# Last pair of a feed-forward stage: the first pair's squares moved behind its first plain chunk, its two token halves swapped, one PSUM bank taken from a fresh tile

## Chip, core and metric

The kernel runs on one core of one Trainium2 chip. The metric is the device time of one execution in microseconds (us). All work is in float32, but TensorE is fed float32r operands: each float32 operand is split into a rounded part ("hi", names `wh`, `act`, and half of `g` and `gs`) and the rest ("lo", `wl`), and a product is made of three matmuls: hi by hi, hi by lo, lo by hi.

## What is computed

One decoder layer on 256 tokens of width 2048. Only its end matters here: a squared-ReLU MLP of width 8192, a normalisation over the row, and a residual sum.

```
u = rms_norm(h, pre_ff_gain[l], NORM_EPS)
f = jnp.square(jax.nn.relu(u @ w_ff1[l])) @ w_ff2[l]
h = h + rms_norm(f, post_ff_gain[l], NORM_EPS)
```

The row's mean square needs all 2048 columns of `f`, so the last step can't begin before the last column block is there.

## The kernel before

Tokens come in two halves of 128 (`t` = 0, 1). The MLP's hidden width is done in four quarters `q`; in each, 16 column chunks of `w_ff1` give `g`, and then `w_ff2` is applied in two passes `fast_pair(ga, q, m)`, each for a pair of column blocks of 512 (block 2m + i, i = 0, 1). So `m` = 0 is the first pair, `m` = 1 the last, and the last pass of all (`q` = 3, `m` = 1) is called closing.

A pass has, along the quarter's hidden width, four chunks `kc` of 512. Chunks `kc` = 0 and 1 are done as a **unit** (`fast_unit`): a 2 x 2 block scheme with seven products, named A1 to A7, in place of eight. A unit takes 42 matmuls: three operand buffers of 12 (A1 and A2, A7 and A3, A5 and A6) and one of 6 (A4). Chunks `kc` = 2 and 3 are done plainly, 24 matmuls each for one column block (`plain_chunk`, 12 for each token half). The closing pass has its own order: unit 0, then the plain chunks (2,0) and (3,0) of column block i = 0, then unit 1, then both plain chunks of block i = 1, token half by token half.

The operands come from HBM into three `raw` buffers of 1 MB (queue of SP, line 134) and from there into three pairs of `wh` and `wl` buffers: ScalarE casts raw to `wh` (L140 a whole chunk, L156 half a buffer of a unit), VectorE subtracts for `wl` (L146, L157). A unit's buffers are partly sums of raw blocks (VectorE, L162). A raw buffer is loaded again as soon as VectorE has read it last.

In every pass but the closing one, the two plain column blocks of the result are copied by ScalarE to `tmp` and added to the total (`acc`, in the trace `y_sb`) by DMAs with accumulation that GpSimd issues (L859); the unit's part goes the same way from `ev` (L816). In the closing pass VectorE adds directly (L814, L833, L866).

`finish(n, t, ...)` takes the square of one 128 x 512 block of the total with its row sum (ScalarE, L873) and then multiplies the block by the gain (VectorE, L876). For the last block it also takes the root (L875) and the reciprocal (L878), and the final loop (L914, one per block) scales, adds the residual, and stores (SP, L916). Before the change the four `finish` calls of the first pair stand in the program right after `fast_pair(ga, 3, 0)`; where each engine runs them is the scheduler's choice, as `finish` doesn't pin its instructions to their place in the program.

Results lie in PSUM tiles `ps` of two banks each. Four tiles, `pa` to `pd`, fill PSUM. In the closing pass the last column block has both halves in the two banks of `pd`: `plain[1, 1]` is bank 0, `plain[0, 1]` is bank 1. Each engine runs its own list in order, and an instruction that waits holds up those behind it.

Of the kernel before, what the change touches and what calls it, by code (L numbers as in the profile page):

```python
# [13 lines left out]
AF = mybir.ActivationFunctionType  # L14
# [6 lines left out]
NT = S // P  # L21
# [16 lines left out]
NQ = 4  # L38
# [8 lines left out]
FAST = 2  # L47
# [8 lines left out]
def tile_layer(ctx, tc, x, x_t, pre, vecs, lams, rope_t, subln, b_conv, post_mix, post_ff,  # L56
               w_q, w_k, w_v, w_cv, w_cg, w_ga, w_gc, w_co, w_o, w_f1, w_f2, out):
    nc = tc.nc
# [46 lines left out]
    pin = tc.keep_in_program_order  # L105
# [103 lines left out]
    def take():  # L209
        if not queue:  # L210
            fill()
        return queue.pop(0)

    def done(refill=True):
        state["live"] -= 1
        if refill:
            fill()
# [34 lines left out]
    def new_ps():  # L252
        pi[0] += 1
        return ps_pools[pi[0] % len(ps_pools)].tile([P, 2, 512], F32, name="ps")
# [497 lines left out]
    acc = y_sb  # L752
# [20 lines left out]
    def fast_pair(ga, q, m):  # L773
# [64 lines left out]
        for kc, i in chunks:  # L838
            if kc < FAST:
                if i == 0:  # L840
                    fast_unit(kc, kc == FAST - 1)
                    if kc == FAST - 1:
                        combine()
                        if closing:
                            first_half()
                continue
            if closing and i == 1:
                continue
            wt = take()
            for t in (1, 0):  # L850
                plain_chunk(kc, i, wt, t)
            done()
            if (kc, i) != [c for c in plains if c[1] == i][-1]:
                continue
            if not closing:
                tmp = evp.tile([P, NT, 512], F32, name="tmp", bufs=2)
                for t in (1, 0):
                    nc.scalar.copy(tmp[:, t], plain[t, i])
                    nc.gpsimd.dma_start(total(t, i), tmp[:, t], accum_op=ALU.add)  # L859
        if closing:  # L860
            wts = [take(), take()]
            for t in range(NT):
                for j in range(2):
                    plain_chunk(FAST + j, 1, wts[j], t)
                with tc.high_priority(offset=CHAIN):
                    nc.vector.tensor_tensor(total(t, 1), plain[t, 1], total(t, 1), op=ALU.add)  # L866
                    finish(2 * m + 1, t, total(t, 1), True)
            done()
            done()

    def finish(n, t, dst, last):
        sq = fin2.tile([P, 2, S], F32, name="z").rearrange("p a t -> p (a t)")
        nc.scalar.activation(sq, dst, AF.Square, accum_out=fss[:, t, n:n + 1])  # L873
        if last:
            nc.scalar.activation(r3[:, t:t + 1], fss[:, t, n:n + 1], AF.Sqrt, bias=fpre[:, t:t + 1], scale=1.0 / D)  # L875
        nc.vector.tensor_tensor(dst, dst, pff[n // 2][:, (n % 2) * 512:(n % 2 + 1) * 512], op=ALU.mult)  # L876
        if last:
            nc.vector.reciprocal(r3[:, t:t + 1], r3[:, t:t + 1])  # L878

    for q in range(NQ):  # L880
        ga = Mixed()
        for j in range(KT // 2):
            ps = ws_pair(u2) if q or j else lead_ps
            z = fin2.tile([P, 2, S], F32, name="z")
            ws_sum(z, ps)
            nc.vector.tensor_tensor(z, z, r2b.unsqueeze(1).to_broadcast([P, 2, S]), op=ALU.mult)
            sc = fin2.tile([P, 8, P], F32, name="sc", bufs=1)
            gg = sc[:, 0:4].rearrange("p (a t) n -> p a (t n)", a=2)
            nc.vector.scalar_tensor_tensor(gg, z, 0.0, z, op0=ALU.max, op1=ALU.mult)
            if j < 2 * FAST:  # L890
                ga.put_fast(j, sc)
            else:
                ga.put_pair(j, gg)
        if q == NQ - 1:
            def again():
                return actp.tile([P, 2, 2 * S], F32R, name="act").bitcast(F32)

            pff = [again().rearrange("p a n -> p (a n)") for i in range(2)]
            for i in range(2):
                nc.gpsimd.dma_start(pff[i], post_ff[i * 1024:(i + 1) * 1024].partition_broadcast(P))  # L900
            h_fin = [again() for n in range(NB)]
            for n in range(NB):
                nc.gpsimd.dma_start(h_fin[n], h_keep[:, :, n * 512:(n + 1) * 512])
        for m in range(NB // 2):
            fast_pair(ga, q, m)
            if q == NQ - 1 and m == 0:
                for n in range(2):
                    for t in range(NT):
                        finish(n, t, acc[:, t, n * 512:(n + 1) * 512], False)
    out_r = out.rearrange("(t p) d -> p t d", p=P)  # L910
    for t in range(NT):
        for n in range(NB):
            ns = slice(n * 512, (n + 1) * 512)
            nc.vector.scalar_tensor_tensor(acc[:, t, ns], acc[:, t, ns], r3[:, t:t + 1], h_fin[n][:, t],  # L914
                                           op0=ALU.mult, op1=ALU.add)
            nc.sync.dma_start(out_r[:, t, ns], acc[:, t, ns])  # L916
# [64 lines left out]
```

## Time and profile before

| | us |
|---|---|
| three runs: median (lowest to highest) | 1551.09 (1549.72 to 1553.07) |
| profiled execution: its own time | 1549.57 |
| profiled execution: span of the trace | 1547.8 |
| TensorE busy in the span | 1524.4 |
| VectorE busy | 1274.6 |
| ScalarE busy | 787.0 |
| GpSimd busy | 41.8 |

The span runs from the first to the last instruction; the execution's own time has 1.8 us more around it. Times in the trace count from the start of the span. The closing pass begins at 1485.3 and the span ends at 1547.8. A busy TensorE row is a matmul in the pipeline: a matmul of 512 columns shows 0.39 us, but the next starts 0.23 us after it.

### The profile page before, as it was taken

How to read it: one execution, taken by the hardware profiler on the slowest of the kernel's cores; microseconds unless marked ns; L12 is line 12 of the kernel's file. 1: busy time of each engine (PE TensorE's matmuls, PEld its weight loads, DVE VectorE, ACT ScalarE, POOL GpSimd, SP SyncE). 2: the span in 40 equal slices, each digit the busy share in tenths (PEclk: the TensorE clock that was granted, in tenths of full speed). 3: DMA queues.
4: the chain of work that ended last, by engine and by line, in shares of the span. 5: the costliest groups of instructions: out<-in, count | busy, mean ns of one | idle time of the engine just before them, and what ended most of it. 6: DMA issues, size and time to landing. Idle time of an engine off the chain costs nothing. (4 is left out here: it accounts for less than half of the span.)

```text
span 1547.8 us, 19432 instructions
## 1 busy us (share of the span) xinstructions
PE 1524.4 (98%) x7734; PEld 1297.3 (84%) x7734; DVE 1274.6 (82%) x1605; ACT 787.0 (51%) x851; POOL 41.8 (3%) x73
## 2 busy tenths in 40 slices
PE   9999999999999999999999999999999999999986
PEld 8888888888888888888887888888888888888865
DVE  7999999999999997956546878867887778867877
ACT  7444454555555545734436545554455445544553
POOL 0000000000000000000000000000011000100010
PEclk9999999999999999999999999999999999999999
DMA  8655555454545555575555754775388546885672
GB/s 305 217 190 189 189 191 188 165 189 164 190 163 178 203 192 192 187 274 188 190 190 172 250 190 167 240 245 189 144 267 268 213 172 195 262 257 189 240 217 95
DMA packets 51484, 313.66 MB, mean 203 GB/s; under 512 B 5825, under 2 KB 5953, under 8 KB 16705
## 3 DMA queue, kind: packets, MB, share of 16 engines
q1 hardware_dynamic: 43920, 289.61, 52.3%
q0 software_dynamic: 7040, 22.02, 6.0%
q8 instruction: 60, 0.98, 0.2%
q10 hardware_dynamic: 432, 0.79, 0.2%
q14 instruction: 32, 0.25, 0.0%
HBM read 295.62 MB, written 4.19 MB: 194 GB/s over the span
## 5 line engine op out<-in xcount | busy, mean ns | idle before, releaser
L140 ACT CAST wh<-raw 128x2048 fp32r<-128x2048 f32 (+2 forms) x260 | 460.8, 1778 | 492.4 <-PE ps L294 162.6
L146 DVE TENSOR_TENSOR wl<-raw,wh 128x2048 fp32r<-128x2048 f32 (+2 forms) x260 | 552.0, 2127 | 192.5 <-ACT wh L140 188.3
L271 PE MATMUL ps<-act,wh 128*128 128x512 f32 x1984 | 479.2, 392 | 0.3 <-ACT wh L140 0.3
L271 PEld LDWEIGHTS ps<-act,wh 128*128 128x128 f32 x1984 | 364.6, 188 | 70.8 <-ACT wh L140 0.6
L275 PEld LDWEIGHTS ps<-act,wl 128*128 128x128 f32 x1984 | 256.6, 191 | 10.0
L275 PE MATMUL ps<-act,wl 128*128 128x256 f32 x1984 | 264.0, 284 | 0.0
L293 PE MATMUL ps<-wl,act 128*128 128x512 f32 x624 | 243.8, 391 | 0.0
L292 PE MATMUL ps<-wh,act 128*128 128x512 f32 x624 | 243.7, 390 | 0.0
L294 PE MATMUL ps<-wh,act 128*128 128x512 f32 x624 | 243.6, 390 | 0.0
L478 DVE SCALAR_TENSOR_TENSOR y_all<-c,vec,y_all 128x256 f32<-128x256 f32 x480 | 210.8, 483 | 0.0
L293 PEld LDWEIGHTS ps<-wl,act 128*128 128x128 f32 x624 | 117.2, 188 | 24.2
L294 PEld LDWEIGHTS ps<-wh,act 128*128 128x128 f32 x624 | 117.2, 188 | 24.1
L292 PEld LDWEIGHTS ps<-wh,act 128*128 128x128 f32 x624 | 117.1, 188 | 23.9
L156 ACT CAST wh<-raw 128x1024 fp32r<-128x1024 f32 x64 | 65.3, 1050 | 91.8 <-PE ps L829 26.0
L828 PE MATMUL ps<-wl,g 128*128 128x512 f32 x256 | 101.5, 397 | 1.1
L827 PE MATMUL ps<-wh,g 128*128 128x512 f32 x256 | 100.0, 390 | 2.2 <-DVE y_sb L866 2.2
L829 PE MATMUL ps<-wh,g 128*128 128x512 f32 x256 | 99.7, 389 | 0.0
L797 PE MATMUL ps<-wh,gs 128*128 128x512 f32 x224 | 87.8, 392 | 5.5 <-ACT wh L156 5.5
L798 PE MATMUL ps<-wl,gs 128*128 128x512 f32 x224 | 87.9, 393 | 0.5 <-DVE wl L157 0.5
L800 PE MATMUL ps<-wh,gs 128*128 128x512 f32 x224 | 87.6, 391 | 0.0
L157 DVE TENSOR_TENSOR wl<-raw,wh 128x1024 fp32r<-128x1024 f32 x64 | 76.4, 1221 | 2.2 <-PE ps L275 1.1
L156 ACT CAST wh<-sum 128x1024 fp32r<-128x1024 f32 x48 | 49.1, 1050 | 38.6 <-PE ps L271 14.3
(200 smaller groups left out, 1257.2 us busy)
## 6 DMA issues: line engine op xcount, KB each, us to landing
raw<-in_w_f_dram SPq DMA_DIRECT2D x124, 1024.0 KB, 5.0
raw<-in_w_q_dram SPq DMA_DIRECT2D x16, 1024.0 KB, 4.9
raw<-in_w_k_dram SPq DMA_DIRECT2D x16, 1024.0 KB, 4.8
raw<-in_w_v_dram SPq DMA_DIRECT2D x16, 1024.0 KB, 4.8
raw<-in_w_ga_dram SPq DMA_DIRECT2D x16, 1024.0 KB, 4.8
raw<-in_w_gc_dram SPq DMA_DIRECT2D x16, 1024.0 KB, 4.8
raw<-in_w_co_dram SPq DMA_DIRECT2D x16, 1024.0 KB, 4.9
raw<-in_w_o_dram SPq DMA_DIRECT2D x16, 1024.0 KB, 4.9
```

Source lines behind the costliest of these rows:

```text
L140: i = nc.scalar.copy(wh[:, a:b], raw[:, a:b])
L146: i = (eng or nc.vector).tensor_sub(wl[:, a:b], raw[:, a:b], wh[:, a:b].bitcast(F32))
L156: nc.scalar.copy(hi, src)
L271: a = nc.tensor.matmul(ps[:, j], wh[:, k * P:(k + 1) * P], acts.both(k), start=(k == 0), stop=False)
L275: a = nc.tensor.matmul(ps[:, j, S:], wl[:, k * P:(k + 1) * P], acts.hi(k), start=False, stop=(k == KT - 1))
L292: nc.tensor.matmul(ps, acts.hi(k, a, b), wh[:, sl], start=(k == 0), stop=False)
L293: nc.tensor.matmul(ps, acts.hi(k, a, b), wl[:, sl], start=False, stop=False)
L294: nc.tensor.matmul(ps, acts.lo(k, a, b), wh[:, sl], start=False, stop=(k == KT - 1))
L478: i = nc.vector.scalar_tensor_tensor(y, c[:, j:j + S], vcol(ct, V_DW + j), y, op0=ALU.mult, op1=ALU.add)
L827: pin(nc.tensor.matmul(ps, ga.hi(k, a, b), wh[:, sl], start=first, stop=False))
L828: pin(nc.tensor.matmul(ps, ga.hi(k, a, b), wl[:, sl], start=False, stop=False))
L829: pin(nc.tensor.matmul(ps, ga.lo(k, a, b), wh[:, sl], start=False, stop=last))
```

## The change

Three edits, all around the closing pass. First, the four `finish` calls of the first pair are made inside the closing pass, after its first plain chunk (2,0), and the squares are pinned to that place. Second, the last column block is done with token half 1 first, and the final loop runs over the halves in the same order. Third, `plain[0, 1]` is a bank of a fresh PSUM tile, which takes the place of `pa` once that has been read.

```
             done()
+            if closing and kc == FAST:
+                for n in range(2):
+                    for t in range(NT):
+                        finish(n, t, acc[:, t, n * 512:(n + 1) * 512], False, pinned=True)
...
         if closing:
+            plain[0, 1] = new_ps()[:, 0]
             wts = [take(), take()]
-            for t in range(NT):
+            for t in (1, 0):
                 for j in range(2):
                     plain_chunk(FAST + j, 1, wts[j], t)
...
-    def finish(n, t, dst, last):
+    def finish(n, t, dst, last, pinned=False):
         sq = fin2.tile([P, 2, S], F32, name="z").rearrange("p a t -> p (a t)")
-        nc.scalar.activation(sq, dst, AF.Square, accum_out=fss[:, t, n:n + 1])
+        i = nc.scalar.activation(sq, dst, AF.Square, accum_out=fss[:, t, n:n + 1])
+        if pinned:
+            pin(i)
...
             fast_pair(ga, q, m)
-            if q == NQ - 1 and m == 0:
-                for n in range(2):
-                    for t in range(NT):
-                        finish(n, t, acc[:, t, n * 512:(n + 1) * 512], False)
     out_r = out.rearrange("(t p) d -> p t d", p=P)
-    for t in range(NT):
+    for t in (1, 0):
```

Lines behind the first edit have other numbers in the changed kernel: L866 is L871, L873 is L878, L876 is L883, L914 is L917.

ScalarE's list, before, from the last casts of unit 0 to those of unit 1. The cast from `sum` that stands alone between two pairs of squares is A4's of unit 0; the two casts of 128 x 2048 are the chunks (2,0) and (3,0); the four casts from `raw` behind them and the three from `sum` are unit 1's.

```order
L156 CAST wh<-sum 128x1024
L873 ACTIVATE z,fss<-y_sb 128x512 x2
L156 CAST wh<-sum 128x1024
L140 CAST wh<-raw 128x2048 x2
L156 CAST wh<-raw 128x1024 x2
L873 ACTIVATE z,fss<-y_sb 128x512 x2
L156 CAST wh<-raw 128x1024 x2
L156 CAST wh<-sum 128x1024 x3
```

The same place in the changed kernel:

```order
L156 CAST wh<-sum 128x1024 x2
L140 CAST wh<-raw 128x2048 x2
L156 CAST wh<-raw 128x1024 x3
L878 ACTIVATE z,fss<-y_sb 128x512 x3
L156 CAST wh<-raw 128x1024
L878 ACTIVATE z,fss<-y_sb 128x512
L156 CAST wh<-sum 128x1024 x3
```

No square stands ahead of A4's cast any more, nor ahead of the two chunks. All four now stand among unit 1's casts: three ahead of the fourth raw cast (operand A7), one behind it.

VectorE's list, before, from the second half of A4's sums to the last subtraction of unit 1; the L876 are the gain products behind the four squares.

```order
L157 TENSOR_TENSOR wl<-sum,wh 128x1024 x2
L876 TENSOR_TENSOR y_sb<-y_sb,act 128x512 x2
L157 TENSOR_TENSOR wl<-sum,wh 128x1024
L146 TENSOR_TENSOR wl<-raw,wh 128x2048 x2
L157 TENSOR_TENSOR wl<-raw,wh 128x1024 x2
L876 TENSOR_TENSOR y_sb<-y_sb,act 128x512 x2
L162 TENSOR_TENSOR sum<-raw 128x1024
L157 TENSOR_TENSOR wl<-raw,wh 128x1024
L162 TENSOR_TENSOR raw<-raw 128x2x512
L162 TENSOR_TENSOR sum<-raw 128x1024
L157 TENSOR_TENSOR wl<-raw,wh 128x1024
L162 TENSOR_TENSOR sum<-sum,raw 128x1024
```

The same place in the changed kernel:

```order
L157 TENSOR_TENSOR wl<-raw,wh 128x1024 x2
L162 TENSOR_TENSOR sum<-raw 128x1024
L162 TENSOR_TENSOR raw<-raw 128x2x512
L157 TENSOR_TENSOR wl<-raw,wh 128x1024
L883 TENSOR_TENSOR y_sb<-y_sb,act 128x512
L162 TENSOR_TENSOR sum<-raw 128x1024
L883 TENSOR_TENSOR y_sb<-y_sb,act 128x512 x2
L157 TENSOR_TENSOR wl<-raw,wh 128x1024
L883 TENSOR_TENSOR y_sb<-y_sb,act 128x512
L162 TENSOR_TENSOR sum<-sum,raw 128x1024
L157 TENSOR_TENSOR wl<-sum,wh 128x1024 x3
```

All four gain products now stand between unit 1's sums and subtractions; before, two stood ahead of A4's subtraction of unit 0 and two ahead of unit 1's first sum.

VectorE's end, before, from the scale of the first three squares' sums on:

```order
L836 TENSOR_SCALAR fpre<-fpre 128x2
L878 RECIPROCAL r_6985<-r_6985 128x1
L914 SCALAR_TENSOR_TENSOR y_sb<-y_sb,r_6985,act 128x512 x4
L866 TENSOR_TENSOR y_sb<-ps,y_sb 128x512
L876 TENSOR_TENSOR y_sb<-y_sb,act 128x512
L878 RECIPROCAL r_6985<-r_6985 128x1
L914 SCALAR_TENSOR_TENSOR y_sb<-y_sb,r_6985,act 128x512 x4
```

And in the changed kernel:

```order
L836 TENSOR_SCALAR fpre<-fpre 128x2
L871 TENSOR_TENSOR y_sb<-ps,y_sb 128x512
L885 RECIPROCAL r_6985<-r_6985 128x1
L917 SCALAR_TENSOR_TENSOR y_sb<-y_sb,r_6985,act 128x512 x4
L883 TENSOR_TENSOR y_sb<-y_sb,act 128x512
L885 RECIPROCAL r_6985<-r_6985 128x1
L917 SCALAR_TENSOR_TENSOR y_sb<-y_sb,r_6985,act 128x512 x4
```

The sum that takes the last half out of PSUM (L866, now L871) moves from behind the first half's four final operations to ahead of them and of their reciprocal. TensorE's list has the same rows in the same order; what its first matmul of the last half waits for is VectorE's L809 (the last reader of `pa`) where it was L866 (the reader of the other bank of `pd`).

## Rows read from the trace of the kernel before

**Rows 1.** The page, part 1: busy us (share of the span) xinstructions.

```profile
PE 1524.4 (98%) x7734; PEld 1297.3 (84%) x7734; DVE 1274.6 (82%) x1605; ACT 787.0 (51%) x851; POOL 41.8 (3%) x73
```

**Rows 2.** Waits from 1485 to 1540: total us, times, longest us.

```profile
PE ps L797 <- ACT wh L156: 5.5, 1, 5.5
...
PE ps L827 <- DVE y_sb L866: 2.2, 1, 2.2
```

**Rows 3.** ScalarE's timeline about unit 0: start us, us, what, [idle before <- releaser].

```profile
1487.58 1.07 ACT L156 CAST wh<-sum 128x1024 fp32r<-128x1024 f32 x1
1496.77 0.63 ACT L873 ACTIVATE z<-y_sb 128x512 f32<-128x512 f32 x1 [8.12 <-DMA y_sb<-tmp]
...
1498.01 1.03 ACT L156 CAST wh<-sum 128x1024 fp32r<-128x1024 f32 x1
```

**Rows 4.** TensorE's timeline: unit 0's first matmul, A4's first, chunk (2,0)'s second.

```profile
1485.26 0.39 PE L797 MATMUL ps<-wh,gs 128*128 128x512 f32 x1
...
1499.09 0.79 PE L797 MATMUL ps<-wh,gs 128*128 128x512 f32 x1 [5.51 <-ACT wh L156]
...
1503.22 0.50 PE L828 MATMUL ps<-wl,g 128*128 128x512 f32 x1
```

**Rows 5.** TensorE's timeline: unit 1's first matmul, chunk (2,1)'s second.

```profile
1514.03 0.39 PE L797 MATMUL ps<-wh,gs 128*128 128x512 f32 x1
...
1524.00 0.50 PE L828 MATMUL ps<-wl,g 128*128 128x512 f32 x1
```

**Rows 6.** Stretches: length, busy us (instructions) by engine, granted clock, DMA share, GB/s.

```profile
1485.00:1493.00 8.00, 8.00 (x37) 6.60 (x36) 5.49 (x5) 3.65 (x5) 3.41 (x4) 1.00 0.99 268
...
1499.00:1503.00 4.00, 3.44 (x7) 2.11 (x7) 3.35 (x2) 3.75 (x4) 0.00 (x0) 0.53 0.00 0
```

**Rows 7.** VectorE's timeline about unit 1.

```profile
1507.56 1.28 DVE L876 TENSOR_TENSOR y_sb<-y_sb,act 128x512 f32<-128x512 f32 x2
1508.76 1.22 DVE L162 TENSOR_TENSOR sum<-raw 128x1024 f32<-128x1024 f32 x1
...
1515.69 3.61 DVE L157 TENSOR_TENSOR wl<-sum,wh 128x1024 fp32r<-128x1024 f32 x3
1521.66 2.29 DVE L146 TENSOR_TENSOR wl<-raw,wh 128x2048 fp32r<-128x2048 f32 x1 [2.36 <-ACT wh L140]
```

**Rows 8.** Issues on the queues of GpSimd and of SP about unit 0.

```profile
1488.14 2.57 POOL L859 DMA_DIRECT2D y_sb<-tmp  x3 [1.65 <-ACT tmp L858]
...
1487.11 1.46 SPq L134 DMA_DIRECT2D raw<-in_w_f_dram  x2
```

**Rows 9.** Issue to landing: tile tmp (last four transfers), tile raw (last seven).

```profile
DMA to landing us min/median/max: 3.5/8.9/10.0
...
DMA to landing us min/median/max: 4.8/5.2/8.1
```

**Rows 10.** DMA queues in 1490 to 1492, and in 1496 to 1498 (packets, MB, share).

```profile
q1 hardware_dynamic: 110, 0.77, 100.7%
...
q0 software_dynamic: 229, 0.41, 112.8%
```

**Rows 11.** VectorE's timeline at the end.

```profile
1528.99 0.69 DVE L809 TENSOR_TENSOR ev<-ps,ev 128x512 f32<-128x512 f32 x1
...
1538.46 0.68 DVE L866 TENSOR_TENSOR y_sb<-ps,y_sb 128x512 f32<-128x512 f32 x1
1539.93 0.69 DVE L876 TENSOR_TENSOR y_sb<-y_sb,act 128x512 f32<-128x512 f32 x1 [0.79 <-ACT z L873]
...
1540.73 2.74 DVE L914 SCALAR_TENSOR_TENSOR y_sb<-y_sb,r,act 128x512 f32<-128x512 f32 x4
```

**Rows 12.** TensorE's timeline: first and last matmul of the last token half.

```profile
1531.79 0.50 PE L827 MATMUL ps<-wh,g 128*128 128x512 f32 x1 [2.21 <-DVE y_sb L866]
...
1537.13 0.39 PE L829 MATMUL ps<-wh,g 128*128 128x512 f32 x1
```

**Rows 13.** ScalarE's timeline: the root for the first token half at the end.

```profile
1535.28 0.29 ACT L875 ACTIVATE r<-fss,fpre 128x1 f32<-128x1 f32 x1 [0.96 <-DVE fpre L836]
```

## Prediction

> **What bounds the kernel now.** The page's busy shares come first [rows 1]: TensorE is busy 98% of the span, so nearly all of it is matmuls at their pace, and the change neither adds nor removes one. It can win only where TensorE stands still, or behind its last matmul. The view of waits, cut to the closing pass, gives both places [rows 2]: one wait of 5.5 us of a unit's matmul for a cast of ScalarE, and one of 2.2 us of a plain matmul for VectorE's L866.
>
> The first is read on ScalarE [rows 3]. Its cast before last for unit 0 begins at 1487.58 and takes 1.07. Then it stands still for 8.12 us, until a DMA from `tmp` into `y_sb` has landed: the next entry in its list is the first square, which reads that total. A4's cast is two entries behind, at 1498.01, and TensorE, which wants A4 next, starts it at 1499.09 after 5.51 us of idleness [rows 4]. The wait costs more than its length: in 1485 to 1493 the granted clock was 1.00, after the idleness, in 1499 to 1503, 0.53 [rows 6], which is about the lower of TensorE's two levels (1.2 against 2.4 GHz).
>
> The second is at the end [rows 12]: the last token half's first matmul starts at 1531.79, 2.21 us after the half before it ended, since L866 had first to read the other bank of the same PSUM tile.
>
> **First term, the squares.** Behind the change no square stands ahead of A4's cast. Unit 1 shows what a unit takes when nothing blocks its casts: from its first matmul at 1514.03 to the second matmul of the chunk behind it at 1524.00 [rows 5], 9.97 us. Unit 0 takes, between the same two points, 1503.22 - 1485.26 = 17.96 [rows 4]. The difference is **8.0 us**: 5.5 of wait, 2.5 of lower clock and late subtraction. I take it whole, since unit 1 has the same 42 matmuls and the same buffers. The chunk's second matmul should come at 1495.2, and unit 1 start at 1514.03 - 7.99 = 1506.0.
>
> **What is late next.** The squares and gain products don't vanish; they now lie in unit 1's preparation. On ScalarE the three squares ahead of A7's cast take about 0.6 us each (two of them fill 1496.77 to 1498.01, 1.24 us [rows 3]). VectorE is the tighter one. In before, its chain for unit 1 runs from 1508.76 to 1515.69 + 3.61 = 1519.30, 10.54 us, and the next subtraction, which waits for a cast anyway, starts at 1521.66 [rows 7]: 7.63 behind unit 1's first matmul. Four products at 1.28 / 2 = 0.64 each [rows 7] make the chain 13.1 us. It begins when raw block (1,1) has landed. That load goes out when the chunk (2,0) has been subtracted; in unit 1's pattern that is 1521.66 + 2.29 - 1514.03 = 9.92 behind the unit's start [rows 5, 7], so at 1495.2 for unit 0. With the median 5.2 to landing [rows 9] the chain runs from 1500.4 to 1513.5. It is due at 1506.0 + 7.6 = 1513.6. So the cover just suffices, with about 0.1 us to spare; I cost the products at **nothing**, and each us that the block lands later costs one us. The bound on that side is the slowest load in the rows, 8.1 [rows 9], which would cost 2.7; on the other, nothing is gained by an earlier landing.
>
> **Do the squares still wait?** The `tmp` transfers are the same; three are issued between 1488.14 and 1490.71 [rows 8], and the slowest takes 10.0 [rows 9], so all have landed by 1500.7 at the latest if nothing more comes between. The first square is now due after a cast that needs chunk (2,0) done on TensorE and block (1,1), at about 1501.6. Two loads that were issued later in before, (1,1) and (2,1), can now come ahead of the transfers. A load of 1 MB moves in about 2.7 us (0.77 MB in 2 us at 100.7% of the engines [rows 10]), so at worst the last total is ready at 1500.7 + 5.4 = 1506.1. A7's cast has to start by about 1507.7 (A7 is due 12 matmuls of 0.23 after 1506.0, the cast takes 1.07) with one square of 0.6 ahead of it: 1507.1 is the limit. Cost: nothing, with 1 us to spare at the worst. A third load, (3,1), waits for A7's subtraction and can't come before it.
>
> **Queues.** DMA traffic of the two queues is weighed here. In 1490 to 1492, when three `tmp` transfers had been issued, the hardware queue (loads) moved 0.77 MB and the software queue has no row; in 1496 to 1498 the software queue has all [rows 10]. So loads were served first, and I let block (1,1) land after the median time. The Trainium skill, DMA: Bandwidth & Descriptors, section "Queues, rings and completion order", says instead that each DMA engine goes round-robin between the queue rows that have work, a packet at a time. By that rule block (1,1) would share the engines with the totals that are left; this stretch of the trace doesn't show such sharing.
>
> **Second term, the end.** The last half's first matmul waits for L809 now, which ends at 1528.99 + 0.69 = 1529.68 [rows 11], where the half before ends at 1531.79 - 2.21 = 1529.58 [rows 12]. So it starts at about 1529.75, 2.05 earlier, and TensorE's last matmul ends at 1535.5 (before: 1537.13 + 0.39 = 1537.5). Not all of this arrives. VectorE must now take L871 (0.68) as soon as TensorE is done, 1535.5 to 1536.2, ahead of the first half's reciprocal; the root is there at 1535.28 + 0.29 = 1535.57 [rows 13]. Then reciprocal 0.2, four final operations 2.74, the product 0.6 and reciprocal 0.2 (the square falls beside the four), four more 2.74 [rows 11], with the gaps between them: 1542.7. Before: 1540.73 + 2.74 = 1543.47. That is **0.7 us**. The bounds are nothing (the order on VectorE eats it) and 2.05 (all of TensorE's gain arrives). I take 0.7, since before has only 0.79 of idle time of VectorE in this stretch to give [rows 11]. The stores behind it, four per half, are of the same number and size.
>
> **Sum.** 8.0 + 0.7 = 8.7 us. The profiled execution took 1549.57; with the change 1540.9. The median of the runs is 1551.09, 1.5 above it, so for a median I forecast 1542.4.
>
> **Rivals.**
> *The loads and totals share the engines.* If block (1,1) lands as the slowest load did (8.1), because the totals take turns with it, VectorE's chain starts 2.9 later, and with the 0.1 to spare TensorE waits 2.7 in or behind unit 1. Gain 6.0: 1545.1. For it: VectorE's slack is a tenth, and the load falls into the last us of the transfers. Against it: [rows 10]; and the 8.1 is of a load that had another ahead of it, 1.1 us older [rows 8]. I give it 2 in 10. It is also what the rule of the Trainium skill, DMA: Bandwidth & Descriptors, would give, and the trace bears that out only by the one slow load.
>
> *The wait comes back under another name.* A4's cast also needs its sum and a free buffer; were one of these late too, the 5.5 would shrink only partly. Say half of the first term and nothing at the end: gain 4.0 or less, 1547 to 1551. Against it: unit 1 has the same conditions and no wait of its A4 shows [rows 2]. This is the rival in which the change doesn't do what it says.
>
> *Slower.* The third square waits for the last total, and A7's cast stands behind it. From a landing at 1507.1 on each us is one us of TensorE's. At 1515.8 the 8.7 are gone, at 1518.9 the kernel is 0.2% slower, 1554.2. It needs the last total to land some 18 us later than 1500.7. Two loads can delay it by 5.4; only transfers starved far beyond what [rows 9] show would do that.
>
> **Chances.** Forecast (gain 7.5 to 10) 0.69; sharing (5 to 7.5) 0.20; the wait comes back (up to 4 or 5) 0.08; slower 0.03. A measurement of this kernel tells about 0.2% (3.1 us) from no change. The forecast, the sharing and a part of the third case (0.03) are beyond it: faster 0.92. The rest of the third is 0.05, same; slower 0.03. Range: at the low end the gain of 8.7 with all 2.05 of the end in place of 0.7, and the run to run spread of about 1.4 below the median seen in the runs, 1551.09 - 10.05 - 1.4 = 1539.6; at the high end the sharing case and a little of that spread, 1546.0.
>
> **What would show it.** Right: no idle time of ScalarE ahead of a square at the end of unit 0; A4's first matmul without a wait, the granted clock 1.00 across 1494 to 1503; unit 0's first matmul to chunk (2,0)'s second in 10.0 us; three squares back to back in unit 1's casts; the last half's first matmul within 0.3 us of the half before; VectorE idle for less than 0.2 between its last product and the last four operations. Wrong: a wait of a unit 1 matmul for L157 (the chain is late) or for L156 with a square waiting on a `tmp` transfer ahead of it (totals late), or a time from TensorE's last matmul to the end that has grown by more than the 2.05 that TensorE gains.

## Result and the profile after

| | before | after |
|---|---|---|
| median of four runs, us | 1551.64 (1549.72 to 1553.07) | 1542.08 (1540.78 to 1542.41) |
| profiled execution, us | 1549.57 | 1542.29 |
| its span, us | 1547.8 | 1540.5 |

The ratio is 0.9938, with a 95% interval of 0.992 to 0.9955. The kernel is faster by 0.6%, and the interval lies clear of 1: 9.6 us by the medians, 7.3 by the two profiled executions. Part 1 of the page after has the same number of matmuls as [rows 1]; TensorE is busy 2.0 us less and the span is 7.3 shorter, so most of what went is standing still.

```profile
PE 1522.4 (99%) x7734; PEld 1294.3 (84%) x7734; DVE 1274.1 (83%) x1605; ACT 786.4 (51%) x851; POOL 41.8 (3%) x73
```

The waits from 1485 to 1540 of after (total us, times, longest us) have neither of the two lines of [rows 2]. In their place stand small ones, and one chain to follow: a matmul of unit 1 waits for a subtraction (L157), and ScalarE and VectorE both wait for a load.

```profile
ACT wh L156 <- DMA raw<-in_w_f_dram: 4.9, 2, 3.2
...
DVE sum L162 <- DMA raw<-in_w_f_dram: 1.7, 1, 1.7
...
PE ps L798 <- DVE wl L157: 1.0, 1, 1.0
...
PEld ps L827 <- DVE ev L809: 0.6, 1, 0.6
```

ScalarE's timeline of after, against [rows 3]: unit 0's last two casts are back to back, nothing stands still ahead of a square, and the first square starts right behind the cast that waited for block (1,1).

```profile
1487.77 2.00 ACT L156 CAST wh<-sum 128x1024 fp32r<-128x1024 f32 x2
...
1502.60 1.05 ACT L156 CAST wh<-raw 128x1024 fp32r<-128x1024 f32 x1 [3.22 <-DMA raw<-in_w_f_dram]
1503.56 0.62 ACT L878 ACTIVATE z<-y_sb 128x512 f32<-128x512 f32 x1
```

TensorE's timeline of after, against [rows 4, 5, 12]: unit 0's first matmul, chunk (2,0)'s second, unit 1's first, A7's second (which waits), chunk (2,1)'s second, the last two halves' border, and the last matmul.

```profile
1485.44 0.39 PE L797 MATMUL ps<-wh,gs 128*128 128x512 f32 x1
...
1495.42 0.50 PE L828 MATMUL ps<-wl,g 128*128 128x512 f32 x1
...
1506.21 0.39 PE L797 MATMUL ps<-wh,gs 128*128 128x512 f32 x1
...
1510.28 0.50 PE L798 MATMUL ps<-wl,gs 128*128 128x512 f32 x1 [0.96 <-DVE wl L157]
...
1517.62 0.50 PE L828 MATMUL ps<-wl,g 128*128 128x512 f32 x1
...
1522.84 0.39 PE L829 MATMUL ps<-wh,g 128*128 128x512 f32 x1
1523.36 0.50 PE L827 MATMUL ps<-wh,g 128*128 128x512 f32 x1
...
1528.72 0.39 PE L829 MATMUL ps<-wh,g 128*128 128x512 f32 x1
```

From such rows come the four legs that everything below is told in, for the first profile of before, for after, and for a second profile of before taken later (last experiment):

| leg, us | before | after | before, second |
|---|---|---|---|
| unit 0's first matmul to unit 1's | 28.77 | 20.77 | 30.12 |
| unit 1's first to chunk (2,1)'s second | 9.97 | 11.41 | 9.97 |
| from there to the last half's first | 7.79 | 5.74 | 7.79 |
| last half's first to VectorE's end | 11.68 | 12.77 | 12.31 |
| sum | 58.21 | 50.69 | 60.19 |

Against the first profile, 8.00 is gained in unit 0, 1.44 given back in unit 1, and 0.96 gained at the end (2.05 less 1.09): 7.52; unit 0 begins 0.18 later, hence 7.3 in the span.

Where the 1.44 comes from is read on VectorE. Against [rows 7] its chain for unit 1 begins at 1502.52 with a wait for a load, and its next subtraction (L146) follows without a gap:

```profile
1502.52 1.23 DVE L162 TENSOR_TENSOR sum<-raw 128x1024 f32<-128x1024 f32 x1 [1.69 <-DMA raw<-in_w_f_dram]
...
1509.00 1.22 DVE L157 TENSOR_TENSOR wl<-raw,wh 128x1024 fp32r<-128x1024 f32 x1
...
1511.87 3.49 DVE L157 TENSOR_TENSOR wl<-sum,wh 128x1024 fp32r<-128x1024 f32 x3
1515.28 2.29 DVE L146 TENSOR_TENSOR wl<-raw,wh 128x2048 fp32r<-128x2048 f32 x1
```

The DMA view of after says why the block was late. Its rows are packets, MB and share of the DMA engines; q1 is the queue of the loads, q0 that of the accumulating transfers, called totals below. The windows are 1487 to 1489, 1489 to 1491, 1491 to 1493, 1493 to 1495, 1495 to 1497 (with the load that is issued there, KB and us to landing), 1497 to 1499, and 1499 to 1501:

```profile
q1 hardware_dynamic: 16, 0.13, 32.4%
...
q1 hardware_dynamic: 89, 0.73, 93.2%
...
q1 hardware_dynamic: 82, 0.54, 94.1%
q0 software_dynamic: 2, 0.00, 1.1%
...
q1 hardware_dynamic: 55, 0.45, 69.7%
...
q0 software_dynamic: 138, 0.25, 69.1%
q1 hardware_dynamic: 46, 0.25, 33.2%
...
raw<-in_w_f_dram SPq DMA_DIRECT2D x1, 1024.0 KB, 7.1
...
q0 software_dynamic: 198, 0.36, 99.4%
q1 hardware_dynamic: 15, 0.12, 15.2%
...
q1 hardware_dynamic: 89, 0.73, 87.3%
q0 software_dynamic: 40, 0.06, 17.3%
```

Block (1,1) goes out at 1495.39 and lands 7.1 us later. From 1489 to 1493 the loads have the engines, as in [rows 10]; but those are the two loads issued at 1487.29 and 1488.4, of which the second lands at 1497.3. Up to 1497 the load queue moves 0.13 + 0.73 + 0.54 + 0.45 + 0.25 = 2.10 MB, which is within rounding these two loads of 1024 KB and nothing of block (1,1). From 1497 to 1499 the three totals issued from 1488.15 to 1490.72 have 99% and the load queue moves 0.12 MB; only then does it get the engines. So the block did not share with the totals: it stood behind them until about 1499.

The end, on VectorE, against [rows 11]: L871 right behind TensorE's last matmul, then the two groups of four.

```profile
1529.14 0.69 DVE L871 TENSOR_TENSOR y_sb<-ps,y_sb 128x512 f32<-128x512 f32 x1 [0.48 <-PE ps L829]
...
1529.94 2.74 DVE L917 SCALAR_TENSOR_TENSOR y_sb<-y_sb,r,act 128x512 f32<-128x512 f32 x4
...
1533.39 2.74 DVE L917 SCALAR_TENSOR_TENSOR y_sb<-y_sb,r,act 128x512 f32<-128x512 f32 x4
```

### The profile page after: what moved, and what is told of

Read it like the earlier page. It is cut to its first block, busy times and chain, and to the rows that moved or that the text cites. A ratio compares the mean times of both kernels' runs of the same rounds, so it can differ in the third digit from the quotient of the medians.

```text
span 1540.5 us, 19433 instructions
## 1 busy us (share of the span) xinstructions
PE 1522.4 (99%) x7734; PEld 1294.3 (84%) x7734; DVE 1274.1 (83%) x1605; ACT 786.4 (51%) x851; POOL 41.8 (3%) x73
## 4 chain that ended last, share of the span: by engine, by line
PE 90%; DVE 4%; ACT 2%; DMA 2%; issue 1%; SPq 0%; DVEq 0%; ACTq 0%
PE ps L271 29%; PE ps L275 15%; PE ps L292 9%; PE ps L294 9%; PE ps L293 9%; PE ps L828 3%; PE ps L829 3%; PE ps L827 3%; DVE wl L146 2%; ACT wh L140 2%; PE ps L798 2%; PE ps L797 2%; PE ps L800 2%; DMA raw<-in_w_f_dram 1%; DMA raw<-in_w_cv_dram 1%
## 5 line engine op out<-in xcount | busy, mean ns | idle before, releaser
L146 DVE TENSOR_TENSOR wl<-raw,wh 128x2048 fp32r<-128x2048 f32 (+2 forms) x260 | 552.0, 2127 | 191.6 <-ACT wh L140 187.2
L157 DVE TENSOR_TENSOR wl<-raw,wh 128x1024 fp32r<-128x1024 f32 x64 | 76.5, 1222 | 3.1 <-ACT wh L156 2.0
```

Of the source, the lines that this page charges most:

```text
L146: i = (eng or nc.vector).tensor_sub(wl[:, a:b], raw[:, a:b], wh[:, a:b].bitcast(F32))
```

## Experiments

The theory to be tested: the squares' wait for the accumulating transfers was the whole first term, and the 1.44 us given back are block (1,1), late behind those transfers, plus four products in the chain behind it. Rivals are with each run. Times are medians and ratios are to the kernel before, which was measured again beside each of the four groups of runs; its medians there were 1551.48, 1551.08, 1550.77 and 1551.30.

### Each part by itself

Only the squares moved, from before: the four calls of `finish` move and their squares are pinned, as in the diff shown ahead of the prediction; the order of the halves and the PSUM tile stay as before. The place of the calls:

```
             done()
+            if closing and kc == FAST:
+                for n in range(2):
+                    for t in range(NT):
+                        finish(n, t, acc[:, t, n * 512:(n + 1) * 512], False, pinned=True)
```

> Only the first edit: the four squares of the first pair move behind chunk (2,0); the last two token halves keep their order and their PSUM tile. Legs are counted from unit 0's first matmul. Theory (the wait for the totals was all of the first term, and VectorE's longer chain in unit 1 gives some back): unit 0's start to chunk (2,0)'s second matmul 10.0 us (before 17.96, after 9.98); unit 1's start to chunk (2,1)'s second matmul 11.4 (before 9.97, after 11.41), as block (1,1) again lands some 7 us after its issue; the last half's start and the end as in before, 7.8 and 11.7 behind. In all 6.6 us faster than before. Rival (the 1.4 that unit 1 lost belongs to the new order at the end, or to the fresh tile): unit 1's leg 10.0 here, 8.0 us faster.

Measured: 1544.36, ratio 0.996 (0.9945 to 0.9975), 7.1 us under before where 6.6 was expected; the profiled execution, 1546.55, is the slowest of its four. Unit 0's leg to unit 1 is 20.79, so the first term is this edit alone. Unit 1's leg is 12.76 where 11.4 was expected: (1,1) landed after 8.5 us this time, not some 7. And the end, not mended here, shows something else: the last half waited as in [rows 12], but its first matmul to TensorE's last took 7.38 where before took 5.73. TensorE's timeline of this run, from its wait on, and its windows 1512 to 1516, behind a wait of A7 of 2.30, and 1524 to 1532 (columns as in [rows 6]):

```profile
1528.00 0.50 PE L827 MATMUL ps<-wh,g 128*128 128x512 f32 x1 [2.17 <-DVE y_sb L870]
...
1529.91 0.63 PE L828 MATMUL ps<-wl,g 128*128 128x512 f32 x1
1530.34 0.63 PE L829 MATMUL ps<-wh,g 128*128 128x512 f32 x1
```

```profile
1512.00:1516.00 4.00, 3.13 (x13) 2.43 (x14) 4.00 (x5) 1.32 (x2) 0.00 (x0) 1.00 0.54 168
...
1524.00:1532.00 8.00, 5.83 (x20) 4.37 (x20) 7.22 (x13) 2.25 (x7) 0.00 (x0) 0.84 0.00 0
```

Some matmuls stand 0.43 apart in place of 0.23, and the granted clock of the second stretch is 0.84: TensorE spent part of it at the lower of its two levels. In the first it stayed at 1.00.

Only the end, from before:

```
         if closing:
+            plain[0, 1] = new_ps()[:, 0]
             wts = [take(), take()]
-            for t in range(NT):
+            for t in (1, 0):
...
-    for t in range(NT):
+    for t in (1, 0):
```

> Only the other two edits: last column block with token half 1 first, the other half's bank in a fresh tile; the squares where they were. Theory: the first legs as in before (17.96 and 9.97), the last half's first matmul 5.7 us behind chunk (2,1)'s second matmul (before 7.79, after 5.74), from there to VectorE's last operation 12.8 (before 11.68, after 12.77); in all 1.0 us faster than before. Rival (all that TensorE gains arrives): 2.05 faster. Rival (the gain at the end came only with the earlier squares): 0.

Measured: 1550.16, ratio 0.9995 (0.9986 to 1.0005), 1.3 us under before; no change lies within the interval. Its last two legs are 5.73 and 12.78, those of after, so the end does what it does in after. Unit 0 to unit 1 took 29.99 here, longer than the 28.77 of before's first profile, so the 1.0 us of the end show in the legs and not in the time.

The end without the fresh tile, from after (halves swapped, both in `pd`):

```
         if closing:
-            plain[0, 1] = new_ps()[:, 0]
             wts = [take(), take()]
```

> The changed kernel without the fresh tile: both halves lie in the two banks of one tile again, half 1 first. Theory (VectorE bounds the end, not TensorE): the last half's first matmul waits for the sum that reads the other bank and starts 0.6 to 0.7 later than in the changed kernel, but VectorE's list here has three final operations of the first half ahead of the second half's sum, which fill the 0.5 us in which it stood idle; its last operation ends 0 to 0.3 us earlier than in the changed kernel. Rival (TensorE's earlier start is what the end lives on): 0.7 later, 0.3 us of the end's 1.0 left.

Measured: 1543.65, ratio 0.9951 (0.9933 to 0.9968). The last half's first matmul waits 0.79 for L870, the leg to it is 6.44 (0.70 more than after), but the one behind it is 12.27 (0.50 less): so by these two legs the tile is worth 0.2 us. The expectation, that VectorE would end up to 0.3 earlier than in after, missed by that; its rival, 0.7 later, missed too. VectorE sets most of the end, and TensorE's earlier start is worth only a little. Unit 1's leg was 13.82: (1,1) landed after 8.3, A7 waited 2.10, and in 1512 to 1516 the granted clock was 0.60.

```profile
1511.78 0.50 PE L798 MATMUL ps<-wl,gs 128*128 128x512 f32 x1 [2.10 <-DVE wl L157]
```

```profile
1512.00:1516.00 4.00, 4.00 (x12) 3.13 (x12) 4.00 (x5) 1.05 (x1) 0.00 (x0) 0.60 0.77 262
```

### Without the last totals

The kernel before without the last quarter's four accumulating transfers:

```
                     nc.scalar.copy(tmp[:, t], plain[t, i])
-                    nc.gpsimd.dma_start(total(t, i), tmp[:, t], accum_op=ALU.add)
+                    if q < NQ - 1:
+                        nc.gpsimd.dma_start(total(t, i), tmp[:, t], accum_op=ALU.add)
```

> The kernel before, with the four accumulating transfers from tmp left out in the last quarter's first pass, so that the totals of its two plain column blocks lack that part. The squares stand where they stood, ahead of A4's cast. Theory (it was the landing of these transfers that ScalarE waited for): no wait ahead of the first square, A4's cast 1.2 us after ScalarE's cast before, no wait of A4's matmul, unit 0's leg 10.0 in place of 17.96, unit 1's leg 10.0; some 8 us faster than before. Rival (the squares and products themselves, or a buffer, held A4 up): the wait shrinks only in part, 2 us or more of it stay.

Measured: 1548.55, ratio 0.9984 (0.9975 to 0.9993). This run did not answer its question. With nothing to wait for in `tmp`, the scheduler moved the squares further ahead on ScalarE, and there the first waited for the other transfer into the total, from `ev`:

```profile
1488.85 0.63 ACT L874 ACTIVATE z<-y_sb 128x512 f32<-128x512 f32 x1 [5.55 <-DMA y_sb<-ev]
```

TensorE then waited 1.78 and 1.56 us in unit 0. What can be taken from it is that unpinned squares may be put ahead of another transfer that they need. Later, on top of the same edit, the squares were held where a wait is due, with dependencies that only set an order (two squares ahead of A4's cast, behind the casts before it):

```
-        nc.scalar.copy(hi, src)
+        c = nc.scalar.copy(hi, src)
         nc.vector.tensor_sub(lo, src, hi.bitcast(F32))
+        if held:
+            tc.add_manual_dep(c.ins, held.pop().name, order_only, reason="place")
+        casts.append(c.ins)
...
+    casts, held = [], []
...
-        nc.scalar.activation(sq, dst, AF.Square, accum_out=fss[:, t, n:n + 1])
+        i = nc.scalar.activation(sq, dst, AF.Square, accum_out=fss[:, t, n:n + 1])
+        if n == 0:
+            tc.add_manual_dep(i.ins, casts[-1].name, order_only, reason="place")
+            held[:] = [i.ins]
```

> The kernel before without the four accumulating transfers of the last q; the squares keep their place on ScalarE, two of them ahead of the cast for chunk A4 and two behind it, by dependencies that only set an order. Left out: the last chunk's share of the totals. Theory (the first term is the squares' wait for the transfers and nothing else): with no transfer to wait for, the two squares cost 2 x 0.62 = 1.2 us of ScalarE's slack; unit 0's leg (its first matmul to chunk (2,0)'s) is 10.0 to 11.2 where before it was 17.96, unit 1's 10.0, the end as before; the time 7 to 8.5 us under before. Rival (the squares hold A4's cast or its high-part buffer up by themselves, or TensorE's clock had fallen for another reason): unit 0's leg stays at 13 or more and the time comes down by under 5 us.

Measured: 1543.20, ratio 0.9953 (0.994 to 0.9965): 7.6 us under before. ScalarE ran all four squares between 1487.67 and 1491.08, two ahead of A4's cast and two behind it, with no gap. Unit 0's first matmul to chunk (2,0)'s second took 11.03, unit 1's leg 9.97. What unit 0 takes above 9.97, 1.06, is one wait for a subtraction of VectorE, and the last half waits as before:

```profile
1495.43 0.50 PE L832 MATMUL ps<-wl,g 128*128 128x512 f32 x1 [1.12 <-DVE wl L146]
...
1524.00 0.50 PE L831 MATMUL ps<-wh,g 128*128 128x512 f32 x1 [2.18 <-DVE y_sb L871]
```

So with the squares near their old place and the transfers gone, 6.9 of the 8.0 come: the long wait was for the transfers, and the 1.1 that stay are a wait for VectorE, which still has the squares' products ahead of that subtraction.

The same transfers left out of after:

> The changed kernel, with the four accumulating transfers from tmp left out in the last quarter's first pass (the totals of its two plain column blocks lack that part). Theory (block (1,1) landed 7.1 us after its issue because these transfers were served beside it): it lands in about 5 us, VectorE's chain for unit 1 starts some 2 us earlier, unit 1 runs without a wait, unit 1's start to chunk (2,1)'s second matmul 10.0 us in place of 11.41; 1.4 us faster than the changed kernel. Rival (the four gain products alone make the chain too long): the load lands earlier or not, the leg stays above 11.

Measured: 1541.63, ratio 0.9935 (0.992 to 0.9949). Block (1,1) landed after 4.9 us, VectorE's chain began at once, and unit 1's leg is 9.98:

```profile
1501.48 1.23 DVE L162 TENSOR_TENSOR sum<-raw 128x1024 f32<-128x1024 f32 x1
```

### The products

After with the four products left out:

```
-        nc.vector.tensor_tensor(dst, dst, pff[n // 2][:, (n % 2) * 512:(n % 2 + 1) * 512], op=ALU.mult)
+        if not pinned:
+            nc.vector.tensor_tensor(dst, dst, pff[n // 2][:, (n % 2) * 512:(n % 2 + 1) * 512], op=ALU.mult)
```

> The changed kernel with the first pair's four gain products left out, so that its two column blocks lack the gain. Theory: VectorE's chain for unit 1 takes 10.4 us, unit 1's leg 10.0 to 10.3 in place of 11.41, 1.2 to 1.4 us faster than the changed kernel, and equal to the run with the products on GpSimd if GpSimd costs VectorE nothing. Rival (the late load alone decides): leg above 11.

Measured: 1542.13, ratio 0.9939 (0.9924 to 0.9953). Here (1,1) was late (6.9 us), and still unit 1's leg is 9.97. So neither the late load (6.9, without products) nor the products (with a load of 4.9) cost anything alone; together they are longer than the slack.

```profile
1503.47 1.23 DVE L162 TENSOR_TENSOR sum<-raw 128x1024 f32<-128x1024 f32 x1 [1.54 <-DMA raw<-in_w_f_dram]
```

This rests on the legs. By the times neither run can be told from after, though both were expected 1.2 to 1.4 us below it: 1541.63 and 1542.13 against 1542.08. In their profiles unit 0 begins at 1486.65 and 1486.63, 1.2 later than in after. Over all profiles here it begins between 1484.40 and 1486.67, and 0.5 to 0.7 apart in two profiles of one and the same kernel; that spread arises ahead of the closing pass and is as large as what a leg gains.

After with the four products on GpSimd, which has nothing to do there:

```
-        nc.vector.tensor_tensor(dst, dst, pff[n // 2][:, (n % 2) * 512:(n % 2 + 1) * 512], op=ALU.mult)
+        (nc.gpsimd if pinned else nc.vector).tensor_tensor(dst, dst, pff[n // 2][:, (n % 2) * 512:(n % 2 + 1) * 512], op=ALU.mult)
```

> The changed kernel with the first pair's four gain products on GpSimd in place of VectorE. Block (1,1) lands late as before, some 7 us after its issue. Theory (the chain is load plus 12.8 us of VectorE's work, 2.4 of it products): VectorE's chain takes 10.4 us, unit 1's leg 10.0 to 10.3 in place of 11.41, 1.2 to 1.4 us faster than the changed kernel. Rival (the late load alone decides): leg above 11. Rival (GpSimd's work slows VectorE's on the same operands): VectorE's operations in the chain longer than 1.22 and 1.14 apart, the leg 10.5 or more.

Measured: 1545.48, ratio 0.9962 (0.9947 to 0.9977), with unit 1's leg at 13.93. Beside GpSimd's four products (8.46 us from 1504.16 on) VectorE's own operations nearly doubled, from 1.23 to 2.3 each. Some 0.8 of the 3.96 that the leg lost is the clock: A7 waited 2.08 here, the granted clock was 0.63 in 1512 to 1516, and VectorE at the end of its chain waited 0.84 for a cast that TensorE held up.

```profile
1503.58 1.23 DVE L162 TENSOR_TENSOR raw<-raw 128x1024 f32<-128x1024 f32 x1
1504.72 2.32 DVE L157 TENSOR_TENSOR wl<-raw,wh 128x1024 fp32r<-128x1024 f32 x1
```

The Trainium skill, SBUF — State Buffer, section "Who interferes with whom", says that a VectorE instruction with two inputs in SBUF contends with a GpSimd instruction that reads SBUF; the trace agrees, 1.23 against 2.32.

### Other places for the squares

One chunk later than in after:

```
-            if closing and kc == FAST:
+            if closing and kc == FAST + 1:
```

> The changed kernel with the squares and products emitted after chunk (3,0) in place of (2,0): squares behind the casts of unit 1's third operand, products among the last subtractions of unit 1. Theory (the sum of VectorE's chain counts, wherever the products stand in it): no wait at operand A7, but the same total chain, so the wait comes back at chunk (2,1)'s subtraction; unit 1's leg 11.2 to 11.5 as in the changed kernel, and the same time within 0.3 us. Rival (only the place ahead of A7's subtraction hurt): leg 10.0 to 10.4, 1.2 us faster than the changed kernel.

Measured: 1542.97, ratio 0.9945 (0.9928 to 0.9961); unit 1's leg is 11.11. A7 doesn't wait, but the chunk behind the unit waits 1.15 for L146: the chain is as long, and is felt at its end.

Two squares earlier: the first column block's two ahead of the completion of chunk (2,0), the other two where after has them:

```
+            if closing and kc == FAST:
+                for t in range(NT):
+                    finish(0, t, acc[:, t, 0:512], False, pinned=True)
             done()
             if closing and kc == FAST:
-                for n in range(2):
-                    for t in range(NT):
-                        finish(n, t, acc[:, t, n * 512:(n + 1) * 512], False, pinned=True)
+                for t in range(NT):
+                    finish(1, t, acc[:, t, 512:1024], False, pinned=True)
```

> After, with the first two squares and their two products emitted ahead of chunk (2,0)'s completion, so that ScalarE squares ahead of the cast that waits for block (1,1) and VectorE multiplies while it waits for that block. Theory (unit 1's loss is the late landing plus four products in one chain behind it): two products of 0.68 us leave the chain, unit 1's leg falls from 11.41 to 10.0 to 10.3 and the end is as after; the time is 1.0 to 1.4 us under after of this call. Rival (the totals of that half are not yet summed when the squares come to the head of ScalarE's queue): the square waits in ScalarE, the casts behind it are late, and unit 1's leg is 11.4 or more; the time is that of after or above it.

And after itself, measured beside it:

> After once more, in one call with the version above, for a comparison of the two on one chip. Theory: 0.993 to 0.995 of before; unit 1's leg 11.0 to 14.0, since it hangs on when block (1,1) lands (6.8 to 8.5 us after its issue in the runs up to here) and on whether TensorE's clock falls in the wait. Rival (the 11.41 is a fixed price, not one of a landing): the leg is within 0.2 us of 11.41.

Measured: 1542.71 (1541.46 to 1543.77) against 1542.72 (1540.09 to 1546.79) for after; ratios to before 0.9949 (0.9936 to 0.9962) and 0.9953 (0.994 to 0.9965). In the traces the two squares and their products lie in the time in which both engines waited for the load, and unit 1's leg is 10.41 against 11.19. VectorE's timeline of the version with two squares earlier:

```profile
1501.14 1.29 DVE L885 TENSOR_TENSOR y_sb<-y_sb,act 128x512 f32<-128x512 f32 x2
1502.74 1.22 DVE L162 TENSOR_TENSOR sum<-raw 128x1024 f32<-128x1024 f32 x1 [0.32 <-DMA raw<-in_w_f_dram]
```

That is 0.8 us by the trace, less than the 1.0 to 1.4 expected, and by the times nothing that can be told: no version here is shown to beat after. The expectation for after itself was not decided by its leg: 11.19 lies in the range of the theory (11.0 to 14.0) and only 0.22 below 11.41, where the rival had it within 0.2. It counts as one more point in the table below.

### Before, profiled again

> The kernel before once more, for a second profile of it: by the two profiles the change is worth 7.3 us, by the medians 9.6, and the profiled execution of before (1549.57) is below its median (1551.64). Theory (in most executions of before TensorE's clock falls in one of its two waits, as in the profiles of the versions that keep one of them): the profile shows a time of 1550.5 or more, and either the last half from its first matmul to TensorE's end takes 7.3 us where it took 5.73, or unit 0 from its first matmul to unit 1's takes 29.9 where it took 28.77, or both; together 1.2 to 2.9 us. Rival (the gap is spread over the whole program or comes from the start): both legs are as in the first profile, within 0.2 us, and the time is again 1549.5 to 1550, or above it with the surplus ahead of unit 0.

Measured: profiled execution 1552.08 (median 1551.49, ratio 1.0001, 0.9991 to 1.0011), span 1550.3. Both legs are longer, as the theory had it (unit 0 to unit 1 30.12, last half to TensorE's end 7.25 in place of 5.73); in sum to VectorE's end 60.19 against 58.21. Its windows from 1499, from 1503 and from 1532 (columns as in [rows 6]):

```profile
1499.00:1503.00 4.00, 2.52 (x5) 1.72 (x6) 3.19 (x4) 4.00 (x4) 0.00 (x0) 0.54 0.11 19
1503.00:1507.00 4.00, 4.00 (x11) 2.71 (x11) 4.00 (x3) 3.75 (x7) 0.00 (x0) 0.60 0.40 129
...
1532.00:1540.00 8.00, 6.34 (x21) 5.12 (x22) 7.24 (x14) 2.25 (x7) 0.00 (x0) 0.79 0.07 27
```

The same windows from 1503 and from 1532 in the first profile of before:

```profile
1503.00:1507.00 4.00, 3.90 (x17) 3.11 (x17) 4.00 (x4) 3.13 (x6) 0.00 (x0) 1.00 0.68 233
...
1532.00:1540.00 8.00, 5.52 (x24) 4.21 (x23) 6.57 (x14) 3.04 (x10) 0.00 (x0) 1.00 0.32 109
```

The clock of 1503 to 1507 and of the last half was 1.00 there; here it is 0.60 and 0.79, after a wait of 5.92 at A4 (5.51 there) and the same 2.21 at the last half.

## Why the prediction was right, and where it was not

The forecast, 1542.4 for a median of 1542.08, is closer than its working, and that is luck: two steps missed by about as much in opposite ways (the products, and the way from profile to median, both below). By the two profiled executions the gain is 7.3, which lies in the prediction's band for its rival "sharing" (5 to 7.5). By its own steps:

**First term, 8.0: right.** Unit 0's leg to chunk (2,0) went from 17.96 to 9.98 and unit 1 starts 8.00 earlier after unit 0. The squares moved alone give it; the transfers taken away instead, with the squares near their place, give 6.9. The granted clock is 1.00 from 1493 to 1503, where it was 0.53 in 1499 to 1503 [rows 6].

**The products at nothing: this is the term that failed, by 1.44.** The chain itself was sized well: 13.1 against 12.8 measured (1502.52 to 1515.28), the load's issue 1495.2 against 1495.39. The step that failed is "So loads were served first", read from [rows 10], and with it the landing after the median 5.2 us: it was 7.1. The loads in the first window of [rows 10] are older ones; a load issued behind the totals came behind them, as the 2.10 MB above show. VectorE's chain was to begin 5.6 us ahead of unit 1's first matmul, and began 3.69 ahead (1506.21 - 1502.52), called its lead here. The sign that the prediction itself named as wrong, a wait of a unit 1 matmul for L157, is there: 0.96 us. That each us of lateness costs one us is what the profiles show that keep all four products in VectorE's chain:

| run, us | landing of (1,1) | lead | unit 1's leg over 9.97 | sum of the two |
|---|---|---|---|---|
| after | 7.1 | 3.69 | 1.44 | 5.13 |
| after again | 6.9 | 3.91 | 1.22 | 5.13 |
| squares one chunk later | 6.8 | 3.99 | 1.14 | 5.13 |
| squares only | 8.5 | 2.34 | 2.79 | 5.13 |
| no fresh tile | 8.3 | 2.54 | 3.85 | 6.39 |
| after without totals | 4.9 | 5.93 | 0.01 | no loss |

So with the four products in the chain, a lead of 5.13 should be just enough (the leads seen are 3.99 and less, and 5.93); the prediction's 5.5 (5.6 with 0.1 to spare) was near it. Only the run without the fresh tile leaves the line, by 1.26, and it is the one of these whose clock fell in unit 1 (0.60). Without products the same lateness (lead 1507.41 - 1503.47 = 3.94) costs nothing.

**The rival "sharing" had the right pair and about the right price, but not the mechanism.** It was priced at 2.7 for a landing of 8.1, and the landings were 6.7 to 8.5 wherever the totals were kept and the squares moved; without the totals it was 4.9. The Trainium skill, DMA: Bandwidth & Descriptors, section "Queues, rings and completion order", has the queues take turns packet by packet. The trace shows both queues moving side by side only in part: an older load and the totals in 1495 to 1497 (46 packets to 138). For block (1,1) it shows no turns: none of it moved up to 1497, and in 1497 to 1499 the load queue moved 15 packets to 198. The rows would fit service by age, where loads issued ahead of the totals or among them move, and a load issued behind them comes behind. No run here tests that.

**The squares do not wait for the totals: right.** ScalarE has no wait for `tmp` in after.

**Second term, 0.7: right in kind, 0.96 in size.** TensorE gains the 2.05 forecast and 1.09 of it goes on VectorE, which took L871 first. Against the second profile of before it is 1.59 (20.10 less 18.51), since before's last half runs at a lower clock there. Of it the fresh tile is 0.2; the rest is put down to the swapped halves by difference, as no run swaps them alone from before.

**From profile to median: wrong, the other way.** I added 1.5 us for a median above the profiled execution, as though it stayed. It did not: after's profile (1542.29) lies at its median. The second profile of before shows what such a surplus can consist of: 1.35 more in unit 0's leg (0.41 of it the longer wait at A4), 0.63 more from the last half's start to the end, both at a granted clock that had fallen (0.60 and 0.79) behind the waits that the change takes away, and 0.5 ahead of unit 0 (it begins at 1485.78). So the profile of after was missed by 1.4 (1540.9 against 1542.29), the surplus by about as much with the other sign, and the median came out right. How often before's executions go the one way or the other is not shown by two profiles; of the three experiments that keep the last half's wait (the squares only, and before without totals, twice), all had the longer last half, 7.33 to 7.38. Nor is it shown why after itself once took 1546.79, 4.1 above its median; a fall of the clock in A7's wait cost 1.26 in the run without the fresh tile, too little for that alone.

**Slower, and the wait under another name:** neither occurred; A4's cast has its sum and buffer in time.

## What to carry to other kernels

When work is moved off a stalled place, price it at its new place with the load it meets there as that load will then be issued: a load that goes out sooner may meet transfers that it used to come after, and a median landing from before does not hold. Put such work where its engine already waits for a load, ahead of that wait, not behind it (0.8 us here by the trace, too little for the times to tell). And a wait of TensorE costs more in some executions than in others, so compare two profiles of before, leg by leg, before a gap to the median is carried over.

## What was not expected of the hardware

A wait of 2.1 to 2.3 us was followed by the lower clock in some executions and not in others: after 2.21 us in before's first profile the next matmuls ran at a granted clock of 1.00 (last half 5.73), after 2.21 in its second at 0.79 over the stretch (7.25); after 2.10 in unit 1 at 0.60, after 2.30 in the run with the squares only at 1.00 (1512 to 1516). Of the eight waits of 2.08 to 2.30 in these profiles (the last half in both profiles of before, with the squares only, and in before without totals twice; A7 with the squares only, without the fresh tile, and with the products on GpSimd), six were followed by the lower clock. And four products on an idle GpSimd were dearer to VectorE than on itself: it lost 1.1 us on each of the four operations beside them, where a product costs it 0.64 [rows 7].
